# Token-major products ordered by contraction block instead of by token half

## The chip, the cores and the metric

The kernel runs on one core of one Trainium2 chip. The metric is device microseconds of one execution. Engines are named as in the profile: PE is TensorE (PEld its weight loads), DVE is VectorE, ACT is ScalarE, POOL is GpSimd, SP is SyncE, which issues most of the DMAs.

## The reference

Two decoder layers over 256 tokens with 2048 features, in float32. Every product of activations with a weight matrix sums over 2048 features (the contraction):

```python
for i in range(DEPTH):                       # DEPTH = 2
    hn = rmsnorm(h, e_norm[j] if i % 2 == 0 else o_norm[j])
    if i % 2 == 0:
        u = hn @ e_w_in[j]                   # HGRN2 and RG-LRU heads, each with a SiLU gate
        ...
        mix = y @ e_w_out[j]
    else:
        u = hn @ o_w_in[j]                   # mLSTM heads, output gate and SiLU gate
        ...
        mix = yc @ o_w_out[j]
    h = h + mix
    pl = rmsnorm(p[i] @ ple_w[i], ple_norm[i])
    h = h + jax.nn.sigmoid(h @ ple_gate_w[i]) * pl
return rmsnorm(h, final_norm)
```

## The kernel before

Products are made to float32 accuracy from parts: each weight and each activation is split into a high part and a remainder (`whi`, `wlo`; both parts of an activation lie in one tile `ahl`), and three matmuls are summed: high by high, high by remainder, remainder by high. Weights stream from HBM once. `load_weights` (L119) loads a piece of 128x1024 into `raw` (SP queue), casts it to `whi` on ACT (L133) and subtracts on DVE to get `wlo` (L134). `raw` has five buffers, `whi` and `wlo` four each, so two calls of `load_weights`, of two pieces each, are held at a time; a cast waits until PE has done with the piece whose buffer it takes.

There are two kinds of products. Feature-major ones (`block`, L157) hold the weights still. Token-major ones, which the change is about, hold the activations still (128 tokens, a token half) and stream 512 columns of weights. One chunk of 512 output columns of all 256 tokens is made by `project_tok` (L193) in four quarters of the contraction, kq = 0 to 3. Each quarter is one call of `quarter_tok` (L217): it loads 512 rows of the weight chunk as two pieces and does 24 matmuls (2 token halves hf x 4 contraction blocks kk of 128 x 3 parts; lines L228, L229, L230). Blocks kk = 0, 1 lie in the first piece, 2, 3 in the second. Each token half sums up in a PSUM bank of its own, `ps[hf]`, over the whole chunk; the banks come in turn from a pool `pm` of three (tile `mm`). So of a chunk's two banks the first has been free for long, and the second is the one in which the previous chunk summed its first token half: whoever reads that half out has to be done before the second bank is written. I call this the hand-over.

`project_two` does the first two chunks of a product interleaved, the second of them in banks of another pool (`mx`), where the input of the last quarter comes late. In all there are 31 token-major chunks, 124 quarters: `ei` (2 chunks, reader L770 on ACT), `ez` (2, L554 and L555), `eo` (4, L418 on DVE), `g0` (4, L430), `ov` (4, L974), `oog` (4, L1094), `oz` (4, L554 and L555), `oo` (4, L418) and `g1` (3, L1144).

In `out_proj` (L411, products `eo` and `oo`) the read-out L418 adds a chunk's half to the hidden state on DVE. `to_features` (L375) then turns the chunk feature-major for the next product: DVE transposes (L380), POOL sends the tile to HBM (L505) and fetches it back permuted with four DMAs (L508), ACT casts it (L396) and DVE makes the remainder (L398). These steps are generators in lanes; `pump()` moves each lane on by one step, once per quarter, after 12 of its 24 matmuls. A scheduler in the recording layer settles each engine's order when the program is built, from the program's text, priorities and its own estimate of times. At run time each engine works through its own list in order.

Of the kernel before, what the change touches and what calls it, by code (L numbers as in the profile page):

```python
# [22 lines left out]
KT = D // P  # L23
# [20 lines left out]
def trunk(ctx: ExitStack, tc: tile.TileContext, a, out):  # L44
    nc = tc.nc
    v, s, gp, te, sy = nc.vector, nc.scalar, nc.gpsimd, nc.tensor, nc.sync
# [14 lines left out]
    last = {}  # L61
# [12 lines left out]
    def pump():  # L74
        with ExitStack() as behind:
            for ins in last.values():
                behind.enter_context(tc.issue_after(ins))
            for lane in list(lanes):
                step(lane)
# [39 lines left out]
    def load_weights(src, pieces=1, queues=(sy,)):  # L119
        parts = []  # L120
        for hf in range(2):
            raw = wp.tile([P, 1024], F32, name="raw", tag="raw", bufs=5)
            hi = wp.tile([P, 1024], F32R, name="whi", tag="whi")
            lo = wp.tile([P, 1024], F32R, name="wlo", tag="wlo")
            n = 1024 // pieces
            for c in range(0, 1024, n):
                r, h, l = (x[:, c:c + n] for x in (raw, hi, lo))
                queues[(hf * 1024 + c) // n % len(queues)].dma_start(out=r, in_=src[:, hf * 1024 + c:hf * 1024 + c + n])
                with ExitStack() as order:
                    order.enter_context(tc.high_priority(offset=400))  # L130
                    if pieces > 1:
                        order.enter_context(tc.issue_after(last["split"]))
                    last["act"] = s.copy(h, r).ins  # L133
                    last["dve"] = v.tensor_tensor(out=l, in0=r, in1=h.bitcast(F32), op=ALU.subtract).ins  # L134
            parts.append((hi, lo))
            pieces = 1
        return parts
# [52 lines left out]
    def tokens(x, k, hf):  # L190
        return x[:, k, hf * P:(hf + 1) * P]

    def project_tok(w, j, act, before=None):  # L193

        ps = [pm.tile([P, 512], F32, name="mm", tag="mm") for _ in range(2)]
        for kq in range(4):
            if before is not None:
                before(kq)
            quarter_tok(w, j, kq, act, ps)
        return ps  # L200

    def project_two(w, act, before):

        ps = [[pool.tile([P, 512], F32, name=name, tag=name) for _ in range(2)]
              for pool, name in ((pm, "mm"), (px, "mx"))]
        for j, kq in ((0, 0), (0, 1), (0, 2), (1, 0), (1, 1), (1, 2), (0, 3), (1, 3)):
            before(kq)
            quarter_tok(w, j, kq, act, ps[j])
            if kq == 3:
                yield ps[j]  # L210
# [6 lines left out]
    def quarter_tok(w, j, kq, act, ps):  # L217

        parts = load_weights(w[4 * j + kq])
        for hf in range(2):  # L220
            for kk in range(4):
                k = kq * 4 + kk
                hi, lo = parts[kk // 2]
                c = (kk % 2) * 512
                ah, al, _ = act[k // 2]
                xh, xl = (tokens(x, k % 2, hf) for x in (ah, al))
                wh, wl = hi[:, c:c + 512], lo[:, c:c + 512]
                te.matmul(ps[hf], xh, wh, start=(k == 0), stop=False)  # L228
                te.matmul(ps[hf], xh, wl, start=False, stop=False)  # L229
                last["pe"] = te.matmul(ps[hf], xl, wh, start=False, stop=(k == KT - 1)).ins  # L230
            if hf == 0:
                pump()

    def newton(y, t, r, yh):
# [176 lines left out]
    def out_proj(hq, w, y, lane):  # L411

        act = {}
        for c in range(4):
            ps = project_tok(w, c, y)
            with tc.high_priority(offset=100):
                for hf in range(2):
                    v.tensor_tensor(out=hq[c][:, hf], in0=ps[hf], in1=hq[c][:, hf], op=ALU.add)  # L418
            start(f"{lane}{c}", to_features(hq[c], c, act, None, lane))
            step(f"{lane}{c}")  # L420
        return act
# [181 lines left out]
    with m0_scope:  # L603
        ew = a["ew"]
        fs, qs, ks = [], [], []
        for g in range(2):
            f = m0.tile([P, 1024], F32, name="f", tag="f")
            k = m0.tile([P, 1024], F32, name="k", tag="k")
# [306 lines left out]
    act = out_proj(hq, a["eo"], y, "fe")  # L915
# [30 lines left out]
    with tc.tile_pool(name="m1", bufs=2) as m1:  # L946
# [143 lines left out]
        for j in range(4):  # L1090
            ps = project_tok(a["oog"], j, acth)
# [10 lines left out]
        for j in range(4):  # L1102
            u = m1.tile([P, 2, 512], F32, name="u", tag="vt", bufs=6)
            gate_tok(a["oz"], j, acth, u)
            for hf in range(2):
                for i in range(2):
                    c = hf * 8 + 2 * j + i
# [28 lines left out]
        act = out_proj(hq, a["oo"], y, "fo")  # L1136
# [54 lines left out]
        for hf, ps in enumerate(quarter(1, [(hf, kq) for hf in range(2) for kq in range(4)])):  # L1191
            pl = pls[3][hf][:, T:2 * T]
            gated(4, ps[hf], hq[3][:, hf, T:2 * T], pl, hf, hf == 0)
            x = hss[:, 4, hf:hf + 1]
# [12 lines left out]
            for g, c, n in ((1, 0, 256), (1, 256, 256), (0, 0, 512), (2, 0, 512), (3, 0, 512)):  # L1207
# [13 lines left out]
                x = on.dma_start(out=out[hf * P:(hf + 1) * P, g * 512 + c:g * 512 + c + n], in_=o).ins  # L1221
# [119 lines left out]
```

## Time and profile before

| | |
|---|---|
| time, median of 3 runs | 1054.6 us (1052.64 to 1055.48) |
| the profiled execution | 1052.53 us, span 1050.8 us |
| PE busy | 1039.7 us, 99% of the span, 5632 matmul records |
| DVE busy | 726.6 us, 69% |
| ACT busy | 588.4 us, 56% |
| POOL busy | 141.8 us, 13% |
| granted TensorE clock | 0.997 |
| HBM | 210 GB/s over the span |

A busy PE is not the same as a PE that starts matmuls as fast as it can: a record of 0.39 us for a matmul of 512 columns overlaps the next ones. The spacing of starts (0.23 us in the stretches shown below) tells whether PE waited.

### The profile page before, as it was taken

Reading aid. Unit: us, or ns where it says so; the run is one execution under the profiler, and the core shown is the slowest. Engines: PE = TensorE matmul, PEld = TensorE weight load, DVE = VectorE, ACT = ScalarE, POOL = GpSimd, SP = SyncE. Lnnn points to the kernel's source line nnn. Section 1 sums busy time; section 2 is a strip of 40 time slices with the busy share of each in tenths; the row PEclk is TensorE's granted clock in tenths of the full one; section 3 lists DMA queues with packets and bytes.
Section 4 is the critical chain, followed back from the end, with each engine's and each line's share of the span. In section 5 each row is a group of like instructions: output and inputs, shape, how many; then the busy total and the mean of one; then the engine's idle time right before and its main releaser. Section 6 shows DMA issues by size and latency. Waiting matters only on the chain.

```text
span 1050.8 us, 15202 instructions
## 1 busy us (share of the span) xinstructions
PE 1039.7 (99%) x5632; PEld 875.8 (83%) x5632; DVE 726.6 (69%) x1075; ACT 588.4 (56%) x885; POOL 141.8 (13%) x166
## 2 busy tenths in 40 slices
PE   9999999999999999999999999999999999999996
PEld 7888888888888888878888888888888888888886
DVE  6757897997886656767544887764457775765676
ACT  7775545869654435565544656654445565444553
POOL 0001232522204311111000000000001113211021
PEclk9999999999999999999999999999999999999998
DMA  9865444545877786787555544555557785888652
GB/s 359 301 206 191 172 165 157 180 152 180 271 250 262 238 249 208 237 274 228 189 194 200 173 153 157 170 161 197 197 187 227 248 265 184 289 244 243 202 181 81
DMA packets 63098, 221.21 MB, mean 211 GB/s; under 512 B 7728, under 2 KB 9008, under 8 KB 63024
## 3 DMA queue, kind: packets, MB, share of 16 engines
q1 hardware_dynamic: 55440, 196.64, 56.1%
q0 software_dynamic: 7152, 23.07, 7.3%
q8 instruction: 44, 0.72, 0.3%
q10 hardware_dynamic: 432, 0.52, 0.1%
q14 instruction: 30, 0.25, 0.1%
HBM read 209.20 MB, written 11.01 MB: 210 GB/s over the span
## 4 chain that ended last, share of the span: by engine, by line
PE 98%; DMA 0%; ACT 0%; DVE 0%; SPq 0%; issue 0%; ACTq 0%
PE mm L228 19%; PE mm L229 19%; PE mm L230 19%; PE mm L164 17%; PE mm L170 9%; PE mx L228 2%; PE mx L230 2%; PE mx L229 2%; PE mm L1176 1%; PE mm L1175 1%; PE mm L1174 1%; PE mx L821 1%; PE nu L1057 1%; PE mm L338 1%; PE mm L339 1%; PE mm L337 1%
## 5 line engine op out<-in xcount | busy, mean ns | idle before, releaser
L134 DVE TENSOR_TENSOR wlo<-raw,whi 128x1024 fp32r<-128x1024 f32 (+1 forms) x363 | 446.9, 1248 | 236.4 <-ACT whi L133 199.1
L133 ACT CAST whi<-raw 128x1024 fp32r<-128x1024 f32 (+1 forms) x363 | 377.6, 1044 | 334.5 <-PE mm L230 227.0
L228 PE MATMUL mm<-whi,ahl 128*128 128x512 f32 x896 | 350.4, 391 | 0.0
L230 PE MATMUL mm<-whi,ahl 128*128 128x512 f32 x896 | 348.7, 389 | 0.0
L229 PE MATMUL mm<-wlo,ahl 128*128 128x512 f32 x896 | 348.6, 389 | 0.0
L228 PEld LDWEIGHTS mm<-whi,ahl 128*128 128x128 f32 x896 | 168.2, 188 | 36.1 <-issue 0.8
L230 PEld LDWEIGHTS mm<-whi,ahl 128*128 128x128 f32 x896 | 168.2, 188 | 35.1
L229 PEld LDWEIGHTS mm<-wlo,ahl 128*128 128x128 f32 x896 | 168.2, 188 | 34.5
L164 PE MATMUL mm<-ahl,whi 128*128 128x512 f32 x768 | 183.1, 390 | 0.0
L164 PEld LDWEIGHTS mm<-ahl,whi 128*128 128x128 f32 x768 | 141.4, 188 | 27.5
L170 PE MATMUL mm<-ahl,wlo 128*128 128x256 f32 x768 | 102.1, 286 | 0.0
L170 PEld LDWEIGHTS mm<-ahl,wlo 128*128 128x128 f32 x768 | 97.2, 191 | 3.6 <-issue 0.4
L505 POOL DMA_DIRECT2D ducn<-w x3 | 1.7, 562 | 332.6 <-DVE w L518 332.6
L228 PE MATMUL mx<-whi,ahl 128*128 128x512 f32 x96 | 37.7, 392 | 0.0
L230 PE MATMUL mx<-whi,ahl 128*128 128x512 f32 x96 | 37.4, 389 | 0.0
L229 PE MATMUL mx<-wlo,ahl 128*128 128x512 f32 x96 | 37.4, 389 | 0.0
L176 ACT COPY sm<-mm 128x256 f32<-128x256 f32 x48 | 17.6, 367 | 31.8 <-PE mm L170 31.8
L959 DVE SCALAR_TENSOR_TENSOR qk<-mg,prm,qk 128x255 f32<-128x255 f32 (+2 forms) x48 | 21.0, 476 | 5.0 <-ACT qk L956 4.7
L228 PEld LDWEIGHTS mx<-whi,ahl 128*128 128x128 f32 x96 | 18.0, 188 | 4.1 <-issue 0.4
L398 DVE TENSOR_TENSOR ahl<-r,ahl 128x128 fp32r<-128x128 f32 x64 | 14.3, 280 | 10.2 <-ACT ahl L396 10.2
L230 PEld LDWEIGHTS mx<-whi,ahl 128*128 128x128 f32 x96 | 18.0, 188 | 3.8
L229 PEld LDWEIGHTS mx<-wlo,ahl 128*128 128x128 f32 x96 | 18.0, 188 | 3.7
(295 smaller groups left out, 898.4 us busy)
## 6 DMA issues: line engine op xcount, KB each, us to landing
raw<-in_ew_dram SPq DMA_DIRECT2D x64, 512.0 KB, 4.3
raw<-in_g_dram SPq DMA_DIRECT2D x56, 512.0 KB, 5.1
raw<-in_eo_dram SPq DMA_DIRECT2D x32, 512.0 KB, 5.1
raw<-in_ov_dram SPq DMA_DIRECT2D x32, 512.0 KB, 4.2
raw<-in_oqk_dram SPq DMA_DIRECT2D x32, 512.0 KB, 4.3
raw<-in_oog_dram SPq DMA_DIRECT2D x32, 512.0 KB, 3.8
raw<-in_oz_dram SPq DMA_DIRECT2D x32, 512.0 KB, 4.1
raw<-in_oo_dram SPq DMA_DIRECT2D x32, 512.0 KB, 4.6
```

What stands on the lines that cost most here:

```text
L133: last["act"] = s.copy(h, r).ins
L134: last["dve"] = v.tensor_tensor(out=l, in0=r, in1=h.bitcast(F32), op=ALU.subtract).ins
L164: last["pe"] = te.matmul(ps, parts[k // 8][0][:, c:c + P], act[k // 2][2][:, (k % 2) * 512:(k % 2 + 1) * 512], start=(k == 0), stop=False).ins
L170: last["pe"] = te.matmul(ps[:, T:2 * T], parts[k // 8][1][:, c:c + P], act[k // 2][0][:, k % 2], start=False, stop=(k == KT - 1)).ins
L176: s.copy(small, ps[:, T:2 * T])
L228: te.matmul(ps[hf], xh, wh, start=(k == 0), stop=False)
L229: te.matmul(ps[hf], xh, wl, start=False, stop=False)
L230: last["pe"] = te.matmul(ps[hf], xl, wh, start=False, stop=(k == KT - 1)).ins
L337: te.matmul(ps, xh, wh, start=(k == 0), stop=False)
L338: te.matmul(ps, xh, wl, start=False, stop=False)
L398: v.tensor_tensor(out=lk[:, hf], in0=src[:, hf], in1=hk[:, hf].bitcast(F32), op=ALU.subtract)
L959: v.scalar_tensor_tensor(dst[:, sh:T], pi[:, 0:T - sh], pc("ccw", k * 16 + b), dst[:, sh:T], op0=ALU.mult, op1=ALU.add)
```

## The change

In the first three quarters of each chunk the two loops are exchanged: for each contraction block both token halves are done, three matmuls in one bank and three in the other, in place of twelve in the first bank and twelve in the second. The last quarter keeps the old order, so that the first half still ends twelve matmuls ahead of the second. `pump()` stays after twelve matmuls. What is computed, the number of instructions, and the order in which each bank sums up its products stay as they were.

```diff
     def quarter_tok(w, j, kq, act, ps):
 
         parts = load_weights(w[4 * j + kq])
-        for hf in range(2):
-            for kk in range(4):
-                k = kq * 4 + kk
...
-            if hf == 0:
+        pairs = [(hf, kk) for hf in range(2) for kk in range(4)]
+        if kq < 3:
+            pairs.sort(key=lambda x: x[1])
+        for n, (hf, kk) in enumerate(pairs):
+            k = kq * 4 + kk
...
+            te.matmul(ps[hf], xh, wh, start=(k == 0), stop=False)
+            te.matmul(ps[hf], xh, wl, start=False, stop=False)
+            last["pe"] = te.matmul(ps[hf], xl, wh, start=False, stop=(k == KT - 1)).ins
+            if n == 3:
                 pump()
```

The changed file has two lines more there, so every later line number is larger by two after (L228 to L230 become L230 to L232, L418 becomes L420).

The first place is PE in the first quarter of `g0`. `mm_4016` and `mm_4017` are the banks of token halves 0 and 1, `whi_4021` and `wlo_4022` the first piece of weights, `whi_4027` and `wlo_4028` the second. Before, the last rows of half 0 and the first of half 1:

```order
L229 MATMUL mm_4016<-wlo_4028,ahl_3699 128x512
L230 MATMUL mm_4016<-whi_4027,ahl_3699 128x512
L228 MATMUL mm_4017<-whi_4021,ahl_3692 128x512
L229 MATMUL mm_4017<-wlo_4022,ahl_3692 128x512
L230 MATMUL mm_4017<-whi_4021,ahl_3692 128x512
```

and after, the first rows of the quarter:

```order
L230 MATMUL mm_4016<-whi_4021,ahl_3692 128x512
L231 MATMUL mm_4016<-wlo_4022,ahl_3692 128x512
L232 MATMUL mm_4016<-whi_4021,ahl_3692 128x512
L230 MATMUL mm_4017<-whi_4021,ahl_3692 128x512
L231 MATMUL mm_4017<-wlo_4022,ahl_3692 128x512
L232 MATMUL mm_4017<-whi_4021,ahl_3692 128x512
```

The first write to the second bank, before it the 13th matmul of the quarter, is the fourth now. The first piece of weights is done with after 12 matmuls in place of 18, and the second is first needed at the 13th in place of the 7th.

The second place is DVE in the first chunk of `ez`, where the attention steps of the layer run beside it: L737 (after: L739) makes the operand `f` of PE's attention tiles L731 (after: L733). Before:

```order
L838 SCALAR_TENSOR_TENSOR tt<-sq,tt 128x512
L177 TENSOR_TENSOR mg<-mm,sm 128x256
L737 TENSOR_TENSOR f<-f,tot_2324 128x16x32
L187 TENSOR_TENSOR mg<-mg,hrs 128x512
L746 COPY A<-mx 32x4x32 x4
L841 TENSOR_TENSOR it<-it,tt 128x1024
L134 TENSOR_TENSOR wlo<-raw,whi 128x1024 x2
```

and after:

```order
L840 SCALAR_TENSOR_TENSOR tt<-sq,tt 128x512
L134 TENSOR_TENSOR wlo<-raw,whi 128x1024
L177 TENSOR_TENSOR mg<-mm,sm 128x256
L739 TENSOR_TENSOR f<-f,tot_2324 128x16x32
L187 TENSOR_TENSOR mg<-mg,hrs 128x512
L748 COPY A<-mx 32x4x32 x3
L134 TENSOR_TENSOR wlo<-raw,whi 128x1024
```

One weight remainder, L134, went ahead of the step that PE's attention tiles need.

The third place is PE in the second chunk of `ez`, where the RG-LRU gates L821 (after: L823) stand in the stream. Before:

```order
L784 MATMUL mx_2662<-vt_652,A_1848 128x128
L821 MATMUL mx_2696<-xc_2027,bw_2505 128x256 x2
L821 MATMUL mx_2701<-xc_2027,bw_2505 128x256 x2
L228 MATMUL mm_2618<-whi_2620,ahl_244 128x512
L229 MATMUL mm_2618<-wlo_2621,ahl_244 128x512
```

and after:

```order
L786 MATMUL mx_2662<-vt_652,A_1848 128x128
L823 MATMUL mx_2696<-xc_2027,bw_2505 128x256 x2
L230 MATMUL mm_2617<-whi_2626,ahl_249 128x512
L231 MATMUL mm_2617<-wlo_2627,ahl_249 128x512
L823 MATMUL mx_2701<-xc_2027,bw_2505 128x256 x2
L232 MATMUL mm_2617<-whi_2626,ahl_249 128x512
```

The gates stand in two pieces now, with two weight matmuls between them. Else the order of PE outside the exchanged loops differs in two spots only (one norm matmul L255 six matmuls later, and the eight transposes L540 ahead of `oo` as two and six in place of four and four). POOL's order is the same, SP's differs in one place. From the first read-out of `eo` to the first of `g0` the lists of DVE and ACT are the same as before.

More of the change, by code (lines that the diff above doesn't have):

```diff
@@ L219, in quarter_tok @@
         parts = load_weights(w[4 * j + kq])
-        for hf in range(2):
-            for kk in range(4):
-                k = kq * 4 + kk
[L223 to L230, printed above, removed]
-            if hf == 0:
+        pairs = [(hf, kk) for hf in range(2) for kk in range(4)]
[3 more added lines that the diff above has]
+            k = kq * 4 + kk
+            hi, lo = parts[kk // 2]
+            c = (kk % 2) * 512
+            ah, al, _ = act[k // 2]
+            xh, xl = (tokens(x, k % 2, hf) for x in (ah, al))
+            wh, wl = hi[:, c:c + 512], lo[:, c:c + 512]
+            te.matmul(ps[hf], xh, wh, start=(k == 0), stop=False)
+            te.matmul(ps[hf], xh, wl, start=False, stop=False)
+            last["pe"] = te.matmul(ps[hf], xl, wh, start=False, stop=(k == KT - 1)).ins
+            if n == 3:
                 pump()
```

## The prediction

> **What bounds the kernel now.** I read the page first, then the waits of PE, then the timeline of PE around the places where the loops are exchanged.
>
> ```profile
> PE 1039.7 (99%) x5632; PEld 875.8 (83%) x5632; DVE 726.6 (69%) x1075; ACT 588.4 (56%) x885; POOL 141.8 (13%) x166
> PE 98%; DMA 0%; ACT 0%; DVE 0%; SPq 0%; issue 0%; ACTq 0%
> ```
>
> The chain of work that ended last is PE for 98% of the span. The waits of PE, who waited for whom, are three in all:
>
> ```profile
> PE st L95 <- POOL ones L90: 1.1, 1, 1.1
> PE mm L338 <- DVE wlo L134: 0.9, 2, 0.7
> PE mm L337 <- ACT whi L133: 0.3, 1, 0.3
> ```
>
> They add up to 2.3 us, and all lie in the first products (L337, L338), before the first line that the change touches. So in this execution no exchanged matmul waited for weights or for a bank. Whether PE is also as dense as it can be shows in the starts of its matmuls (first column: start in us, second: duration). These rows are the middle of the last quarter of `eo`, where PE goes from the first bank to the second, and then the first quarter of `g0`:
>
> ```profile
> 390.85 0.39 PE L230 MATMUL mm<-whi,ahl 128*128 128x512 f32 x1
> 391.08 0.39 PE L228 MATMUL mm<-whi,ahl 128*128 128x512 f32 x1
> ...
> 393.57 0.39 PE L230 MATMUL mm<-whi,ahl 128*128 128x512 f32 x1
> 393.80 0.39 PE L228 MATMUL mm<-whi,ahl 128*128 128x512 f32 x1
> ...
> 394.48 0.39 PE L228 MATMUL mm<-whi,ahl 128*128 128x512 f32 x1
> ...
> 396.52 0.39 PE L228 MATMUL mm<-whi,ahl 128*128 128x512 f32 x1
> ```
>
> From 393.80 to 396.52 twelve matmuls take 2.72 us, 0.227 each. The start after the bank change, at 391.08, comes 0.23 after its predecessor too; so does the one after the change of chunk, at 393.80. A change of bank costs nothing that shows. PE is the bound and has no gap to give back here; the change can gain almost nothing in this execution, and the question is whether it opens a gap.
>
> **The change part by part.** *The same matmuls in another order.* The three quarters of 31 chunks, 93 in all, change banks seven times inside instead of once, 93 x 6 = 558 changes more. At the cost just read, nothing: 0 us. The weight loads are one for each matmul as before.
>
> *Weights.* The second piece of a quarter is needed six matmuls later (6 x 0.227 = 1.36 us), and the first piece's buffer comes free 1.36 us sooner. Both help whoever loads them, but no wait of PE stands there to be removed: 0 us here, and up to the difference between this execution and the others in a bad one (below).
>
> *The hand-over.* The second bank of a chunk is written at its 4th matmul instead of its 13th, so the read-out of the previous chunk's first half loses nine matmuls of cover, 9 x 0.227 = 2.04 us. This is the part that decides. I compared, for each chunk, the end of that read-out with the 4th start of the next chunk. In `oz` the tightest is
>
> ```profile
> 809.79 0.69 DVE L555 SCALAR_TENSOR_TENSOR u<-u,mm 128x512 f32<-128x512 f32 x1 [0.37 <-ACT u L554]
> 811.85 0.39 PE L228 MATMUL mm<-whi,ahl 128*128 128x512 f32 x1
> ```
>
> It ends at 810.48 and is needed at 811.85: 1.37 us left, no wait. The products `ov`, `oog` and `oo` have more. In `ei` the read-out waits for the norm:
>
> ```profile
> 39.67 1.27 ACT L770 ACTIVATE vt<-mm,rcr 128x512 f32<-128x512 f32 x2
> 40.38 0.39 PE L228 MATMUL mm<-whi,ahl 128*128 128x512 f32 x1
> ```
>
> The first of the two ends at about 40.3, the bank is needed at 40.38: between 0 and 0.2 us; I take 0.1. The tight product is `eo`, where the read-out L418 stands on DVE behind the remainders L398 of the previous chunk's way through HBM:
>
> ```profile
> 326.43 0.68 DVE L418 TENSOR_TENSOR hq<-mm,hq 128x512 f32<-128x512 f32 x1
> 349.43 0.68 DVE L418 TENSOR_TENSOR hq<-mm,hq 128x512 f32<-128x512 f32 x1
> 371.78 0.68 DVE L418 TENSOR_TENSOR hq<-mm,hq 128x512 f32<-128x512 f32 x1
> 394.35 0.70 DVE L398 TENSOR_TENSOR ahl<-r,ahl 128x128 fp32r<-128x128 f32 x3 [3.48 <-ACT ahl L396]
> 394.97 0.68 DVE L418 TENSOR_TENSOR hq<-mm,hq 128x512 f32<-128x512 f32 x1
> ```
>
> The first three L418 are the first halves of chunks 0 to 2, the last is that of chunk 3. They come 23.0, 22.4 and 23.2 us apart. PE makes a chunk in 96 x 0.227 = 21.8, so they fall behind by 3.3 us in three chunks. The needs:
>
> ```profile
> 350.96 0.39 PE L228 MATMUL mm<-whi,ahl 128*128 128x512 f32 x1
> 372.72 0.39 PE L228 MATMUL mm<-whi,ahl 128*128 128x512 f32 x1
> ```
>
> Chunk 1's half is read out by 350.11 (needed at 350.96: 0.85 left), chunk 2's by 372.46 (needed at 372.72: 0.26 left), chunk 3's by 395.65. That one is needed at 394.48, the fourth start in `g0` above: late by 1.17. Before, it was needed at 396.52, with 0.87 to spare; that cover is gone. A wait also costs a little at its end:
>
> ```profile
> 6.05 0.50 PE L338 MATMUL mm<-wlo,ahl 128*128 128x512 f32 x1 [0.29 <-DVE wlo L134]
> 6.39 0.39 PE L339 MATMUL mm<-whi,ahl 128*128 128x512 f32 x1
> ```
>
> The start behind it comes 0.34 later in place of 0.23, so 0.11 more: 1.17 + 0.11 = 1.28 us. The chain that feeds L418 does not hang on PE there: L396 on ACT waits for the DMA,
>
> ```profile
> 393.92 0.41 ACT L396 CAST ahl<-r 128x256 fp32r<-128x256 f32 x1 [4.30 <-DMA r<-dfe]
> ```
>
> and DVE's list from there to L418 is unchanged; so a PE that stands still does not push it back further. Behind the waiting matmul PE has the rest of `g0` queued, and nobody but the weight casts waits for that. For the same chain the loss at this place is bounded by the cover removed, 2.04 + 0.11 = 2.15; below, by nothing, if the chain runs 1.2 us earlier. [...]
>
> *Steps that the scheduler moved.* One remainder L134 stands on DVE ahead of L737 now:
>
> ```profile
> 216.15 0.68 DVE L737 TENSOR_TENSOR f<-f,tot 128x512 f32<-128x512 f32 x1
> ```
>
> The next pair of remainders, and PE's tiles that use `f`:
>
> ```profile
> 219.90 3.21 DVE L134 TENSOR_TENSOR wlo<-raw,whi 128x1024 fp32r<-128x1024 f32 x2
> ```
>
> ```profile
> 218.61 0.39 PE L230 MATMUL mm<-whi,ahl 128*128 128x512 f32 x1
> 218.93 0.76 PE L731 MATMUL mx<-f,k 128*32 128x32 f32 x64
> ```
>
> `f` is ready at 216.83 and needed at 218.93, 2.10 of cover. The two L134 took 3.21, 1.6 each, so with the moved one 0.5 of cover remains. Between 0 and 0.3; I take 0.1. The gates L821 are split:
>
> ```profile
> 242.96 0.58 PE L228 MATMUL mm<-whi,ahl 128*128 128x512 f32 x1
> 243.38 0.39 PE L229 MATMUL mm<-wlo,ahl 128*128 128x512 f32 x1
> ```
>
> After such small products the first start comes 0.42 before the next in place of 0.23, 0.19 more; going into them costs up to 0.09 (218.61 to 218.93 above). One excursion more, 0.19 to 0.28: I take 0.25. The transposes L540 are two groups as before: 0.
>
> *The sum:* 1.28 + 0.1 + 0.1 + 0.25 = 1.73, say 1.7 us. The bounds are 0 + 0 + 0 + 0.2 = 0.2 and 2.15 + 0.2 + 0.3 + 0.3 = 2.95. The profiled execution took 1052.53 (span 1050.8 and 1.7 around it), so it would take 1054.2. It is quicker than all three runs shown (median 1054.6), 2.1 below the median; carried to the median, 1054.6 + 1.7 = 1056.3.
>
> **The rivals.** *Slower: the way through HBM gets longer.* The casts come in pairs with a pause now:
>
> ```profile
> 387.20 1.05 ACT L133 CAST whi<-raw 128x1024 fp32r<-128x1024 f32 x1 [3.02 <-PE mm L230]
> 388.56 1.06 ACT L133 CAST whi<-raw 128x1024 fp32r<-128x1024 f32 x1 [0.31 <-PE mm L230]
> ```
>
> After, buffers come free every twelve matmuls (2.7 us), so the weight DMAs spread over the pause in which the hidden state's way through HBM could run undisturbed. Its parts landed in
>
> ```profile
> DMA to landing us min/median/max: 3.3/6.9/7.6
> ```
>
> If each of a chunk's two trips came 0.5 us later, well inside that spread, three chunks would bring the last L418 3 us further back: 1.28 + 3 + 0.45 = 4.7 us, 1059.3. It passes 0.3% of the time (3.2 us, about what a measurement of this kernel tells from no change) from 1.5 us in all, 0.25 a trip. Against it: smoother traffic may as well shorten the trips, and the bytes are the same. With whatever else is late in a stage that I found covered, I give 0.32.
>
> *Weights were the hidden cost.* The other runs are up to 2.9 us longer than the profiled one. If that is PE waiting for weights, the 1.36 us of slack on both sides removes much of it. The tightest piece in `g0`,
>
> ```profile
> 398.90 1.21 DVE L134 TENSOR_TENSOR wlo<-raw,whi 128x1024 fp32r<-128x1024 f32 x1
> 400.82 0.39 PE L229 MATMUL mm<-wlo,ahl 128*128 128x512 f32 x1
> ```
>
> is ready 0.71 ahead of its use and would have 2.07. Gaining 2.1 and paying 0.4 gives 1054.6 - 1.7 = 1052.9. For more than 3.2 it would also have to beat the best execution seen. I give 0.11, about half of it beyond 0.3%.
>
> *Changing banks is not free, or slows the clock.* If each of the 558 changes cost the 0.09 us of a change into other tiles, 50 us, 1105. The rows at 391.08 and 393.80 speak against it, and the chance is 0.05. [...] Here the granted clock is
>
> ```profile
> 393.80:571.70 177.90, 177.90 (x804) 145.00 (x803) 106.76 (x135) 95.13 (x130) 13.94 (x29) 1.00 0.69 220
> ```
>
> 1.00 (third figure from the end) in a stage that already changes banks every twelve matmuls. [...] That the loops are not exchanged at run time can be left out, since PE's list shows them exchanged.
>
> **How the numbers follow.** Forecast: one new wait at the head of `g0`, some tenths elsewhere, 1056.3 (own range 1054.8 to 1057.6), chance 0.52, all of it within 0.3%. With half of the weights case: same 0.57. Slower: 0.32 + 0.05 = 0.37. Faster: 0.06. The range goes from the weights case, 1052.9, to the longer trips at 1059.3 with the other small bounds on top, 1061.
>
> **What would show it.** Right: PE's waits list a new line, the bank matmul of `g0` (L230 after) waiting 1 to 2 us for DVE's L420, once, near 394; starts 0.227 apart elsewhere; clock 1.00. Wrong: several waits of that kind in `eo`, or the last first-half L420 over 1 us later than 394.97 plus what PE lost before (longer trips); waits for L134 or L133 (weights); starts above 0.23 at each bank change.

## The result, and the profile after

The changed kernel took 1061.61 us, median of 6 runs (1059.54 to 1067.66), against 1053.74 us for the kernel before (6 runs, 1052.56 to 1055.98): ratio 1.0079, interval 1.0062 to 1.0096. The profiled execution took 1061.44, span 1059.7, which is 8.9 us more than the one before. The forecast was 1056.3, its range ended at 1061. PE's waits, by line:

```profile
PE mm L339 <- ACT pl L349: 2.1, 1, 2.1
PE mm L230 <- DVE u L557: 2.0, 2, 1.8
PE mm L339 <- DVE u L557: 1.7, 1, 1.7
...
PE mx L823 <- ACT sq L790: 0.6, 1, 0.6
PE mm L231 <- DVE wlo L134: 0.6, 1, 0.6
```

All five lines are new; the one that I had forecast (for L420 in `g0`) is not there. The granted clock is 0.997 as before. How far each matmul lags behind its counterpart can be read from the starts of the same matmul in the two timelines; between these places the lag does not change by more than 0.02 (in the table, "new" is what the lag grew by since the row above):

| matmul | start before | start after | lag | new |
|---|---|---|---|---|
| first of `ei` | 17.94 | 18.12 | 0.19 | 0.19 |
| `ez` chunk 2, second quarter | 245.90 | 247.00 | 1.10 | 0.91 (gates) |
| `eo` chunk 3 of 4, first | 350.28 | 352.29 | 2.01 | 0.91 (weights) |
| `oz` chunk 3, second quarter | 816.61 | 819.22 | 2.61 | 0.60 (hand-over) |
| `oz` chunk 4, second quarter | 838.37 | 843.05 | 4.68 | 2.07 (hand-over) |
| first of `oo` | 866.44 | 875.41 | 8.97 | 4.29 (embedding) |
| last of the program | 1041.80 | 1050.75 | 8.95 | 0 |

So 6.96 of 8.95 us arise between 811 and 875 us, in `oz` and in the embedding product (L339 to L341) behind it, and the other stages hold their pace: the 558 extra bank changes cost nothing.

In `oz` the gated tile goes through HBM too, by `feature_major` (L515): POOL sends it out (L507, before L505) and fetches it back (L510, before L508), and ACT scales what comes back (L527, before L525). The ways out on POOL, two of the three before and all three after (first column start, then duration):

```profile
794.83 0.56 POOL L505 DMA_DIRECT2D ducn<-w  x1 [300.88 <-DVE w L518]
798.57 2.19 POOL L508 DMA_DIRECT2D r<-ducn  x4 [3.18 <-DMA ducn<-w]
817.05 0.56 POOL L505 DMA_DIRECT2D ducn<-w  x1 [16.28 <-DVE w L518]
820.90 2.19 POOL L508 DMA_DIRECT2D r<-ducn  x4 [3.29 <-PE mm L230]
```

```profile
797.86 0.56 POOL L507 DMA_DIRECT2D ducn<-w  x1 [298.42 <-DVE w L520]
803.47 2.19 POOL L510 DMA_DIRECT2D r<-ducn  x4 [5.05 <-PE mm L232]
822.18 0.56 POOL L507 DMA_DIRECT2D ducn<-w  x1 [16.52 <-DVE w L520]
827.10 2.19 POOL L510 DMA_DIRECT2D r<-ducn  x4 [4.36 <-issue]
846.51 0.56 POOL L507 DMA_DIRECT2D ducn<-w  x1 [17.22 <-DVE w L520]
852.44 2.19 POOL L510 DMA_DIRECT2D r<-ducn  x4 [5.37 <-DMA ducn<-w]
```

From one start to the next the way out takes 3.7 and 3.9 us before, 5.6, 4.9 and 5.9 after. From the start of the way out to the last landing of the way back I call it a trip: 9.7, 10.5 and 10.8 us before, 13.1, 13.6 and 14.1 after. (Some releasers in brackets name PE or nothing; by the landings, 3.1, 3.2 and 3.2 us after the issue before and 5.0, 4.3 and 5.4 after, POOL waits for the landing each time.) The weight casts on ACT show what changed beside it, before and after:

```profile
793.69 1.06 ACT L133 CAST whi<-raw 128x1024 fp32r<-128x1024 f32 x1 [2.44 <-PE mm L230]
795.05 1.06 ACT L133 CAST whi<-raw 128x1024 fp32r<-128x1024 f32 x1 [0.30 <-PE mm L230]
799.13 1.05 ACT L133 CAST whi<-raw 128x1024 fp32r<-128x1024 f32 x1 [3.02 <-PE mm L230]
```

```profile
794.34 1.06 ACT L133 CAST whi<-raw 128x1024 fp32r<-128x1024 f32 x1 [1.08 <-PE mm L232]
797.06 1.05 ACT L133 CAST whi<-raw 128x1024 fp32r<-128x1024 f32 x1 [1.66 <-PE mm L232]
799.78 1.05 ACT L133 CAST whi<-raw 128x1024 fp32r<-128x1024 f32 x1 [1.67 <-PE mm L232]
```

Two casts 1.4 us apart and a pause of 4.1 became one cast every 2.72 us, and behind each one, with its remainder, a `raw` buffer comes free for the next load, which SP issues, in `oz` in both traces, 0.03 us behind the end of the remainder. SP's list shows where these loads fall. Around the first trip, which starts at 794.83 before and at 797.86 after, it issued

```profile
791.17 0.33 SPq L128 DMA_DIRECT2D raw<-in_oz_dram  x1
792.31 0.33 SPq L128 DMA_DIRECT2D raw<-in_oz_dram  x1
796.03 0.33 SPq L128 DMA_DIRECT2D raw<-in_oz_dram  x1
```

before, and after

```profile
793.18 0.33 SPq L128 DMA_DIRECT2D raw<-in_oz_dram  x1
794.32 0.33 SPq L128 DMA_DIRECT2D raw<-in_oz_dram  x1
796.97 0.33 SPq L128 DMA_DIRECT2D raw<-in_oz_dram  x1
```

Before, no load is issued in the 2.5 us ahead of the way out and the 1.2 us behind its start; after, one is issued 0.9 us ahead of it. What the late return does is seen on ACT, DVE and PE around the second hand-over, after:

```profile
835.88 0.91 ACT L527 ACTIVATE xr<-r,prm 128x256 f32<-128x256 f32 x2 [4.52 <-DMA r<-ducn]
836.70 0.67 ACT L556 ACTIVATE u<-mm,rth 128x512 f32<-128x512 f32 x1
...
837.39 0.69 DVE L557 SCALAR_TENSOR_TENSOR u<-u,mm 128x512 f32<-128x512 f32 x1 [4.78 <-ACT u L556]
...
838.14 0.50 PE L230 MATMUL mm<-whi,ahl 128*128 128x512 f32 x1 [1.75 <-DVE u L557]
```

ACT stands for 4.52 us at L527 for the DMA. The read-out L556 is behind it in ACT's list, DVE's half of it behind that, and PE's fourth matmul of the chunk behind that. In the kernel before the same steps were

```profile
828.65 1.30 ACT L525 ACTIVATE xr<-r,prm 128x256 f32<-128x256 f32 x3
...
830.78 0.67 ACT L554 ACTIVATE u<-mm,rth 128x512 f32<-128x512 f32 x1
```

with no wait for the DMA: the trace has the last part landing at 827.55, 1.1 us ahead of L525. At the embedding it is the third trip, and there not only L556 but also the embedding's own read-outs L349 come late:

```profile
860.74 0.51 ACT L527 ACTIVATE xr<-r,prm 128x256 f32<-128x256 f32 x1 [5.56 <-DMA r<-ducn]
861.16 0.67 ACT L556 ACTIVATE u<-mm,rth 128x512 f32<-128x512 f32 x1
...
862.60 0.50 PE L339 MATMUL mm<-whi,ahl 128*128 128x512 f32 x1 [1.71 <-DVE u L557]
...
865.91 0.57 ACT L349 COPY pl<-mm 128x512 f32<-128x512 f32 x1
...
866.53 0.50 PE L339 MATMUL mm<-whi,ahl 128*128 128x512 f32 x1 [2.05 <-ACT pl L349]
```

### The profile page after: what moved, and what is told of

It is laid out like the page before. It is cut to its first block, busy times and chain, and to the rows that moved or that the text cites. A ratio compares the mean times of both kernels' runs of the same rounds, so it can differ in the third digit from the quotient of the medians.

```text
span 1059.7 us, 15201 instructions
## 1 busy us (share of the span) xinstructions
PE 1041.8 (98%) x5632; PEld 875.9 (83%) x5632; DVE 729.3 (69%) x1075; ACT 588.5 (56%) x885; POOL 141.0 (13%) x166
## 5 line engine op out<-in xcount | busy, mean ns | idle before, releaser
L134 DVE TENSOR_TENSOR wlo<-raw,whi 128x1024 fp32r<-128x1024 f32 (+1 forms) x363 | 450.7, 1256 | 242.7 <-ACT whi L133 211.6
L230 PE MATMUL mm<-whi,ahl 128*128 128x512 f32 x896 | 350.6, 391 | 2.0 <-DVE u L557 2.0
L232 PE MATMUL mm<-whi,ahl 128*128 128x512 f32 x896 | 348.9, 389 | 0.0
L230 PEld LDWEIGHTS mm<-whi,ahl 128*128 128x128 f32 x896 | 168.2, 188 | 39.0 <-DVE u L557 2.9
L232 PEld LDWEIGHTS mm<-whi,ahl 128*128 128x128 f32 x896 | 168.2, 188 | 34.9
L507 POOL DMA_DIRECT2D ducn<-w x3 | 1.7, 562 | 332.1 <-DVE w L520 332.1
L230 PE MATMUL mx<-whi,ahl 128*128 128x512 f32 x96 | 37.7, 392 | 0.0
L232 PE MATMUL mx<-whi,ahl 128*128 128x512 f32 x96 | 37.4, 389 | 0.0
L230 PEld LDWEIGHTS mx<-whi,ahl 128*128 128x128 f32 x96 | 18.0, 188 | 4.1 <-issue 0.4
L232 PEld LDWEIGHTS mx<-whi,ahl 128*128 128x128 f32 x96 | 18.0, 188 | 3.8
L177 DVE TENSOR_TENSOR mg<-mm,sm 128x256 f32<-128x256 f32 x48 | 19.9, 417 | 0.1
```

Of the source, the lines that this page charges most:

```text
L177: v.tensor_tensor(out=dst, in0=ps[:, 0:T], in1=small, op=ALU.add)
```

## The experiments

Times of a group of runs are compared with the kernel before on the same chip. In the first group that kernel itself took 1059.75 us (31 runs, 1052.66 to 1068.27), so there only ratios, waits and trips are used, and the ranges in us that the expectations name cannot tell the theories apart; why that chip is slower with the old order is not known. The theories: **the pause** (weight loads that are spread meet the trip through HBM, which holds up ACT and so PE), and **the cover** (the earlier write of the second bank is what costs).

**The exchange with the weights' old timing.** The blocks of a quarter in the order 0, 2, 3, 1: the bank is still written at the fourth matmul, but the pieces come free at the 18th and 24th.

```diff
-            pairs.sort(key=lambda x: x[1])
+            pairs.sort(key=lambda x: (0, 2, 3, 1).index(x[1]))
```

> The exchange stays, but the four contraction blocks of a quarter go in the order 0, 2, 3, 1, so that the two pieces of weights are needed at the 1st and 7th matmul and come free at the 18th and 24th, as before the change; the second bank is still written at the 4th matmul of the chunk. Theory of the pause (the spread weight loads collide with the way through HBM in oz): each trip of ducn takes 10 to 11 us again in place of 13 to 14, ACT is not held up, no wait at the embedding; only the lost cover stays, so 1054 to 1056 us. Theory of the cover (writing the second bank nine matmuls earlier is the cost by itself): the waits for the read-out of oz stay, 2.7 us and what follows at the embedding, 1058 to 1062 us.

1058.46 us, ratio 0.9976 (0.9940 to 1.0013): no slower than the kernel before on that chip, with all 93 quarters exchanged. In us it lies in the range that I gave to the cover, as the kernel before does on that chip; but PE waited for no read-out at the hand-overs in `oz`, only at the embedding (L557 2.2, L349 1.1), so the cover alone is not the cost. The ways out took 4.9, 4.6 and 5.1 us, between the two kernels, the trips 12.0, 12.7 and 15.0, the last of them longer than in the changed kernel. I had expected 10 to 11. Around the first trip SP issued its loads at the same distances as in the kernel before (3.7 and 2.5 us ahead, 1.2 behind), and the way out still took 4.9 in place of 3.7: something else lengthened it in that execution.

**Only `oz` exchanged**, 12 quarters of 93.

```diff
-        if kq < 3:
+        if kq < 3 and w is a["oz"]:
```

> The loops are exchanged in the product oz alone, 12 of the 93 quarters. Theory of the pause: oz is where the time goes, the trips of ducn take 13 to 14 us, PE waits 0.6 + 2.1 us at the hand-overs and 4.3 us at the embedding: 7 us over the kernel before, about 1060.7. Rival (a sum of small costs all over, or a shift of 2 us that arrives from earlier products): under 3 us, below 1057.

1062.65 us, ratio 1.0045 (1.0008 to 1.0082), all ten runs at 1058.7 or above. The ways out took 4.8, 6.6 and 5.6 us, the trips 12.6, 15.3 and 12.1, and PE waited 3.4 us for L557, 0.4 for L349. These 12 quarters alone make the kernel slower on this chip.

**All but `oz`.** The same line with `is not`.

> The loops are exchanged everywhere but in oz, 81 of the 93 quarters. Theory of the pause in oz: what is left is the wait at the gates L823 (0.9 us) and the one for a weight remainder in eo (0.9 us) with 0.2 at the start, about 1055.7, and no wait between 800 and 875 us. Rival (the later stall comes from what is upstream of oz): about 1060.

1055.42 us, ratio 0.9991 (0.9943 to 1.0040): the other 81 quarters show no loss at this resolution. The expectation that no wait would be left between 800 and 875 us did not hold where a trace can tell: the profiled execution was the longest (1069.47), and in it, with `oz` in the old order, the ways out took 7.4, 3.9 and 6.2 us, the trips 17.1, 14.5 and 16.6, and PE waited 8.4 us for L557. The kernel before took up to 1068.27 here. So on this chip long trips in `oz`, and the waits behind them, came without the exchange in `oz` too; what made them long there is open.

**First quarter in the old order, second and third exchanged.**

```diff
-        if kq < 3:
+        if 0 < kq < 3:
```

> The first quarter of each chunk keeps the old order, the second and third are exchanged: the second bank is written at the 13th matmul again, but the weight loads still spread in the second and third quarter, where both legs of the trip of ducn lie. Theory of the pause: the trips stay at 12 to 14 us and ACT is still held up by them; with the cover back the hand-overs in oz cost 0 to 0.7 us, and the embedding's 4.3 us stay: 1057 to 1060. Theory of the cover: all of it goes, 1054 to 1055.

1059.94 us, ratio 1.0003 (0.9962 to 1.0044), which says nothing by itself; the profiled run waited for L557 for 3.9 us at the embedding and 1.4 us in `oz`, for L349 0.7. The cover was back and did not help: ACT stood at L527 for 4.9 and 6.1 us at the second and third trip, in the changed kernel for 4.5 and 5.6. Its trips are in the table below.

**The changed kernel again**, on another chip.

> The changed kernel itself, beside the others. The kernel before turned out to vary from 1052.7 to 1068.3 us where these experiments run, so both theories need their comparison on one chip. Theory of the pause: its executions all lie at 1058 or above, the kernel before has part of its executions below 1056. Rival (a difference of the moment, not of the kernel): the same spread as before.

1063.99 us (1060.06 to 1067.11) against 1054.11 (1052.69 to 1060.30): 1.0081 (1.0058 to 1.0105). Its trips took 13.3, 15.9 and 13.4 us. The loss belongs to the kernel, on this chip and on that of the result.

**The later casts.** The scaling of a returned chunk is put behind the next chunk's read-outs on ACT, first in the kernel before, then in the changed one:

```diff
-        yield from across(w, r, f"du{gain}{first}", 3)
+        yield from across(w, r, f"du{gain}{first}", 4 if ro else 3)
...
+            if ro:
+                late.enter_context(tc.issue_after(ro["act"]))
```

`ro["act"]` is the last L556 recorded when the step is written out. On ACT's list L527 then follows both read-outs of the next chunk.

> The kernel before, with one thing moved: in oz the casts L525 of a chunk that came back through HBM are put on ACT behind the read-outs L554 of the next chunk, in place of ahead of them. Theory of ACT being held up: an overdue trip no longer delays a read-out, the slow executions of the kernel before go (their waits for DVE u at the hand-overs and at the embedding), so all lie near 1053 to 1056. Rival (the trip itself costs, whatever stands behind it): the spread of before stays.

1053.71 us (1052.33 to 1054.74) against 1054.11 (up to 1060.30), ratio 0.9991 (0.9980 to 1.0002). The median is the same within the interval; its longest run is 5.6 us below that of the kernel before.

> The changed kernel with the same move on ACT. Theory of ACT being held up: the trips of ducn still take 13 to 14 us, but the waits of 0.6 + 2.1 us at the hand-overs in oz and most of the 4.3 us at the embedding go; what stays is 0.9 us each at the gates and in eo: 1054 to 1057. Theory of the cover: the hand-over waits stay, 1057 or more.

1054.70 us (1053.02 to 1056.71), ratio 1.0000 (0.9988 to 1.0012), beside 1063.99 for the changed kernel without it. Here is the same hand-over on ACT:

```profile
832.66 0.69 ACT L559 ACTIVATE u<-mm,rth 128x512 f32<-128x512 f32 x1 [1.67 <-PE mm L232]
...
836.33 0.69 ACT L559 ACTIVATE u<-mm,rth 128x512 f32<-128x512 f32 x1
836.91 1.30 ACT L530 ACTIVATE xr<-r,prm 128x256 f32<-128x256 f32 x3
```

(L559 and L530 are L556 and L527 of the changed kernel.) The trips are as long as ever, 14.8, 14.2 and 12.3 us, and the cover is as short as ever; yet DVE has read out the three halves in `oz` 1.7 to 1.8 us before the fourth matmul, and none of PE's waits in `oz` or at the embedding is left. So it is neither the trip nor the cover by itself but ACT standing at L527 that costs. At the two hand-overs the lost cover has its part in it: beyond what PE had lost before, the read-outs of the changed kernel ended 1.75 and 3.31 us later than those of the kernel before, and the old margins (1.37 + 2.04 = 3.41 and 1.45 + 2.04 = 3.49) would just have held them. The loss at the embedding needs no lost cover: with the first quarter in the old order it came too. What is left are the two other waits:

```profile
PE mm L231 <- DVE wlo L134: 0.8, 1, 0.8
PE mx L828 <- ACT sq L795: 0.6, 1, 0.6
```

**Only the first quarter exchanged.**

```diff
-        if kq < 3:
+        if kq == 0:
```

> Only the first quarter of each chunk is exchanged: the second bank is written at the 4th matmul, as in the changed kernel, but in the second and third quarter, where both legs of the trip lie, the weight pieces come free at the 18th and 24th matmul as before. Theory of the pause: the trips are as in the kernel before, the cost is the lost cover alone, 0 to 1.5 us over the kernel before in its good executions, with part of the executions below 1056. Theory of the cover: all executions at 1058 or above, as in the changed kernel.

1062.64 us (1060.88 to 1065.54), ratio 1.0079 (1.0056 to 1.0102). The number is the one that I gave the theory of the cover; the trips show why it can still belong to the pause:

| kernel | way out, us (POOL, L507 to L510) | way back, us (L510 to the last landing) |
|---|---|---|
| before | 3.7, 3.9, 3.7 | 5.9, 6.6, 7.0 |
| before with later casts | 3.7, 3.9, 3.9 | 8.0, 8.4, 7.1 |
| first quarter old, others exchanged | 4.8, 3.9, 4.6 | 9.0, 10.7, 10.1 |
| only the first quarter exchanged | 4.8, 7.7, 7.1 | 7.2, 6.7, 6.5 |
| changed | 5.6, 4.9, 5.9 | 7.5, 8.7, 8.2 |
| changed with later casts | 6.3, 6.9, 5.8 | 8.5, 7.3, 6.4 |
| changed, half loads in `oz` | 4.1, 3.8, 4.5 | 6.3, 5.9, 8.8 |

In the kernel before, the way out begins at the end of a chunk's first quarter or up to 0.4 us behind it, so it meets the loads that this quarter released. In the table it takes 4.8 to 7.7 at full traffic with that quarter exchanged, and 3.7 to 4.8 with that quarter in the old order. It is a tendency and not a rule: the last kernel below, with that quarter exchanged, had 6.0, 3.9 and 4.9, and all but `oz`, with it in the old order, had up to 7.4 on the first chip. My expectation had put both legs into the second and third quarter; that was wrong. The way back scatters too much for so clear a reading.

**Half the weight traffic in `oz`.** In the changed kernel, each piece in `oz` is loaded by half, and cast and remainder read the half twice:

```diff
+                    sy.dma_start(out=raw[:, 0:512], in_=src[:, hf * 1024:hf * 1024 + 512])
+                    r = raw[:, 0:512].unsqueeze(1).to_broadcast([P, 2, 512])
```

> The changed kernel, but in oz each piece of weights is loaded by half only (256 KB in place of 512 KB) and the cast and the remainder read the loaded half twice; so oz multiplies by wrong weights, with the same matmuls, casts, remainders and buffers. What is tried is the traffic alone. Theory of the pause (the trip of ducn is long because weight loads share the DMA engines with it): both legs shrink, 3.5 us or less to HBM and 6 or less back, ACT is not held up, no wait of PE for u or pl: 1053 to 1056. Rival (the trip is long for POOL's or HBM's own latency, or PE waits for the cover): trips stay at 13 or more, 1059 or above.

1056.87 us (1054.46 to 1058.58), ratio 1.0025 (1.0011 to 1.0039). The first two trips fell to 10.5 and 9.7 us (13.1 and 13.6 in the changed kernel), and PE's waits in `oz` went. The time is above the range that I gave (1053 to 1056). The third trip, beside which the full-sized loads of the embedding begin, stayed at 13.3, and so did one wait:

```profile
PE mm L344 <- ACT pl L354: 2.0, 1, 2.0
```

(L344 and L354 are L339 and L349 of the changed kernel.) So the weight traffic beside a trip lengthens it: where half of it was taken away the trips were short and the waits gone, and where it wasn't both stayed. That the exchange brings more of this traffic into the trip is read from SP's loads and from the table, with the exceptions named.

**The gain products on DVE.** The other new wait, 0.91 us in `eo`, has this behind it in the changed kernel:

```profile
341.79 6.46 DVE L134 TENSOR_TENSOR wlo<-raw,whi 128x1024 fp32r<-128x1024 f32 x1 [1.50 <-ACT whi L133]
342.10 5.05 POOL L374 TENSOR_TENSOR pl<-pl,row 128x512 f32<-128x512 f32 x4
...
348.30 0.50 PE L231 MATMUL mm<-wlo,ahl 128*128 128x512 f32 x1 [0.61 <-DVE wlo L134]
```

A remainder that takes 1.2 us in 341 of its 363 records here took 6.46 while POOL ran four multiplications by the gain of layer 1. The next two kernels do these on DVE:

```diff
-                gp.tensor_tensor(out=pl, in0=pl, in1=rows[g // 2][...], op=ALU.mult)
+                v.tensor_tensor(out=pl, in0=pl, in1=rows[g // 2][...], op=ALU.mult)
```

> The kernel before with the later casts in oz, and with the eight multiplications by the gain of layer 1 (L374) on DVE in place of POOL. Theory (a DVE instruction stands still while POOL's L374 run, which makes an L134 in eo late): the wait of PE for wlo near 347 us (0.8 us) goes and no L134 near there takes over 1.5 us: 1053.0, 0.7 below the kernel with the later casts alone, and the best of all. Rival (the wait there is a weight load or a cast that is late): it stays, and eight more steps of 0.7 us on DVE make eo's hand-over late instead: 1054 or above.

1052.94 us (1052.19 to 1053.95) against 1053.58 (1052.15 to 1060.30), ratio 0.9992 (0.9983 to 1.0001). At that place,

```profile
344.45 2.58 DVE L134 TENSOR_TENSOR wlo<-raw,whi 128x1024 fp32r<-128x1024 f32 x2 [2.25 <-ACT whi L133]
```

two remainders take 1.3 us each, and PE's wait is gone; only waits in the first 10 us are left. It has the lowest median of all the kernels, by less than can be told from no change; none of its 11 runs is above 1053.95, of the 28 of the kernel before eight are.

**The changed kernel without its three costs**: later casts, gain on DVE, `ez` in the old order.

```diff
-        if kq < 3:
+        if kq < 3 and w is not a["ez"]:
```

> The changed kernel with the later casts in oz, with L374 on DVE, and with the loops left in the old order in ez. If the three places found (oz, eo, the gates in ez) are all that the change costs, none of the waits for u, pl, wlo near 347 us or sq is left, and it stands with the kernel before without its own waits: 1052.8 to 1053.5. Rival (a cost of the exchange that is spread over the 87 quarters, which no wait shows): 1054.5 or above.

1053.56 us (1052.18 to 1058.66) against 1053.58, ratio 1.0005 (0.9992 to 1.0019). None of the waits named is left, so no cost that the interval could show is spread over the other 87 quarters. Two of its 12 runs took 1058.3 and 1058.7; why was not tried.

## Why the prediction was wrong

The sum had the sign right, a slower kernel, and that was luck: the wait it rested on did not come, and what came lay where the sum had nothing.

**The bank changes and the clock** (0 us): right; the lag holds through the exchanged quarters, and the granted clock is 0.997 in both. **The hand-over in `ei`** (0.1 us): nothing came; the 0.19 us in the first row of the table arise ahead of it.

**The hand-over.** The step that failed is the reading of `oz`: "1.37 us left, no wait". The margin is right for that execution (1.37 and 1.45 at the two later chunks), but I took the end of the read-out as fixed. In `eo` I followed the chain back behind L418; in `oz` I stopped at L554 and did not look at what stands ahead of it on ACT: L525, which waits for a DMA, with 1.1 us of slack at the second and third trip. The trips became 3.1 to 3.4 us longer, so the first-half read-outs came 1.75 and 3.31 us late, past the margin. This term was 0 in the sum and measured 2.67; with the embedding, which has no line in the sum at all, 6.96.

**The hand-over at the head of `g0`** (1.28 us, the largest term): did not come.

```profile
393.41 0.68 DVE L420 TENSOR_TENSOR hq<-mm,hq 128x512 f32<-128x512 f32 x1
...
396.49 0.39 PE L230 MATMUL mm<-whi,ahl 128*128 128x512 f32 x1
```

The read-out ended 2.40 us before the fourth start. In that execution `eo`'s trips took 13.8 to 13.9 us for the first three chunks, where the execution before had 14.4, 15.2 and 16.0, and PE had lost 2.0 us until then. In the other kernels told of here that exchange `g0`'s first quarter, the margin there was between 0.07 and 2.4 us; only in the one without `oz` exchanged did PE wait there, 0.3 us. One execution's 1.17 was inside the scatter of the trips, and I treated it as a property of the program.

**Weights** (0 us, "Both help whoever loads them"): half of it. No wait for a weight was removed, since there was none. But when a piece comes free is also when a load starts, and there the earlier release did harm. The slower rival named this mechanism exactly, the loads that "spread over the pause", and gave it 0.32, but placed it in `eo` and priced it at 4.7 us. In `eo` the way out took 6.1 to 6.7 us before and 5.6 to 6.3 after: by their length, I take it, no leg there had lain in a pause, so there was nothing to lose; no run tried this. The place with short undisturbed legs, 3.7 to 3.9 us, was `oz`, and the row that would have told it (POOL's L505 and L508) I had not read. During the three ways out the weights' queue moved 0.61, 0.45 and 0.48 MB before and 1.02, 0.81 and 1.29 MB after, which is 163, 117 and 128 GB/s against 182, 165 and 217. With half as many bytes loaded in `oz`, the first two ways out fell from 5.6 and 4.9 us to 4.1 and 3.8. How the one traffic delays the other was not shown.

**The attention operand in `ez`** (0.1 us): no wait came. **The split gates** (0.25 us): mis-sized, 0.91. The excursion of 0.28 is in it; the other 0.63 is a wait that I did not price, because I looked for moved steps on DVE only:

```profile
241.12 1.03 ACT L133 CAST whi<-raw 128x1024 fp32r<-128x1024 f32 x1
242.05 0.58 ACT L787 COPY o<-mx 128x512 f32<-128x512 f32 x1
...
243.73 1.13 PE L823 MATMUL mx<-xc,bw 128*128 128x256 f32 x4 [0.63 <-ACT sq L790]
```

A weight cast went ahead of the read-outs that free the gates' bank: the first of them, L788 before and L790 after, began at 240.88 before and at 242.53 after. With `ez` in the old order the wait is gone.

**The remainder in `eo`** (0.91 us): not foreseen. It is not the exchange's alone: the kernel before with later casts has the same wait (0.8 us), while the kernel before as profiled and the one with only `oz` exchanged have not. But all seven traces with the second and third quarters of `eo` exchanged, and the products on POOL, have it (0.4 to 0.9 us). Where DVE's remainder met POOL's products differed by less than a microsecond: in the kernel before as profiled a remainder began 0.79 us ahead of the first of them and took 1.22, in the changed kernel one began 0.31 ahead and took 6.46.

## What to carry to other kernels

For every read-out that PE will need sooner, look at what stands ahead of it in its engine's list, and whether that waits for a DMA; the margin to price is the smaller of the read-out's own and that of the DMA. Where a load waits for its buffer, as here, a change in when buffers come free is a change in when loads are issued: list the short transfers on the way, and see which of them run in a pause of the loads that the change fills. Work that waits for a DMA belongs behind the work that frees a bank that PE waits for, if nobody needs it sooner; here that took back 9 us (1063.99 to 1054.70).

## What the runs showed of the hardware that was not expected

A tensor-tensor operation on DVE, 1.2 us in 341 of its 363 records, took 6.46 us while four multiplications ran on POOL back to back (5.05 us), and the wait went when these moved to DVE. In the changed kernel's trace it ended 1.10 us behind the last of the four (348.25 and 347.15), and 6.46 is about its own 1.2 and their 5.05: as I read it, it stood still through all four. What held it was not shown. Eight of the traces show it, with 6.3 to 6.7 us; in each the record of the remainder begins 0.1 to 0.6 us ahead of the first multiplication.

512 KB on their way to HBM took 3.7 to 3.9 us between the starts on POOL in the kernel before, where the weight loads moved 0.45 to 0.61 MB in that time, 4.9 to 5.9 us in the changed kernel, where they moved 0.81 to 1.29 MB, and up to 7.7 us with only the first quarter exchanged.
